# Moving the shift columns of the first gate product into its rows, spreading norm factors without diagonals, and a second spread for the final scaling

## The chip, the cores and the metric

One core of one Trainium2 chip runs the whole program; seven cores are idle. The metric is the device time of one execution in microseconds (us). The engines are named as in the profile: PE is TensorE (PEld its weight loads), DVE VectorE, ACT ScalarE, POOL GpSimd, SP SyncE, which here only issues DMAs.

## The reference

Two layers of a trunk run over 256 latent rows `h` and 256 context rows `hc` of width 2048. Layer 0 mixes by centred pooling, layer 1 by neighbourhood attention in which the latent queries also read the context. Every sub-layer begins with an RMS norm and a modulation, and each layer ends with a gated MLP of width 5504. After layer 1 only the latents go on.

```
def rms_norm(x, g):
    y = x * rsqrt(mean(x * x, axis=-1) + 1e-6)
    return y * g
def modulate(x, shift, scale):
    return x * (1 + scale) + shift
def conv_ffn(u, w_gate, w_up, conv_w, conv_b, w_down):
    gp = pad(u @ w_gate)
    gte = gp[:, :T] * conv_w[0] + gp[:, 1:T + 1] * conv_w[1] + gp[:, 2:] * conv_w[2] + conv_b
    return (silu(gte) * (u @ w_up)) @ w_down
...
h = h + ml[:, 2] * y_lat
h = h + ml[:, 5] * conv_ffn(modulate(rms_norm(h, norm2_g[i]), ml[:, 3], ml[:, 4]), ...)
...
return rms_norm(h, final_norm_g)
```

## The kernel before

**Layout.** The rows live in SBUF transposed: `hl` is [128, 16, 256], the 16 slices k being the 2048 features and the 256 columns the latent tokens (T = 256); `hc` is the same for the context. Every fp32 product is split: an operand x becomes hi = x rounded to FP32R and lo = x - hi, and a weight tile w is multiplied as w_hi by [x_hi | x_lo] (512 columns) and w_lo by x_hi (256 columns). Weights come in halves of 1024 columns. For each, SP issues a DMA into a staging tile, ACT casts the hi part (L150) and DVE, at times POOL, subtracts the lo part (L153). The hi and lo tiles of layer 1's MLP take turns in eight pairs of buffers, so a cast waits for the last product that read the same buffer eight halves earlier.

**Order.** The code is written as one stream. A scheduler that simulates the engines' times sets the order in which each engine's queue holds its instructions. `tc.high_priority()` and `tc.issue_after(x)` bend it, and the list `hold` puts weight casts behind named instructions. Each engine takes its queue in order.

**Norm factors.** The class `Norm` serves five norms: n1 and n2 in layer 0, n3 (latents and context, four chunks of 128 tokens) at the start of layer 1, n4 (latents) ahead of layer 1's MLP and n5 (latents) at the end. `add` squares a slice on ACT (L359) and sums up on DVE (L365). `totals` (L378) sums over partitions on PE with a column of ones, which gives one column per chunk with the token in the partition; DVE adds the partial sums (L382) and scales (L383); POOL raises to the power -1/2 (L387). `spread` then has to turn this column into a row that stands in all partitions: DVE multiplies the identity by the column, which makes a diagonal matrix `n4d` (L393), and PE multiplies it with a 128x128 matrix of ones (L395) into a PSUM bank `n4b`. `each` does the whole for n3, n4 and n5; `rstd` for n1 and n2.

**Layer 1's MLP, first block.** While the factor of n4 is being made, PE multiplies the first gate tile g_0 with raw rows, that is `hl` times (1 + scale) without the factor (`raw[k]`, made by L1015 on ACT and L1016 on DVE): 16 products of 512 columns (L1084) and 16 of 256 (L1088). The factor is applied to the result afterwards. The shift's share of g_0 is a column of its own. `shift_sums` multiplies the hi and lo weights with `sh` (the shift as hi and lo, two columns, made by L1021 and L1022) in 32 products of two columns (L1100), and DVE adds both columns into `gsh` (L1102). `norm_b` makes the normed rows `B[k]` (in the tiles `oA`) for all other products: DVE multiplies by the factor (`nrmB`, L1030); ACT casts hi (L1031); for even k DVE makes lo (L1037); for odd k ACT makes a copy `nrmBz` (L1034), and POOL makes lo from it (L1035). PE goes on with u_0, g_1 and u_1 over B[0], B[1] and so on.

**The attention's last stretch.** `x_tile` (L1424) makes the attention's output rows, `oA`, hi on ACT and lo on DVE. In the same stretch POOL copies bias rows (L1345) and multiplies for the rotary embedding (`rk`, `rq`, L1272).

**The end.** The last down product adds into `hl` (L1160, DVE). n5 squares each slice, and `final_gain` (L1132, ACT) multiplies it by the final gain, for the last four slices after n5's spread in the code. `rs` (L1193, ACT) is a copy of the factor for POOL, which scales slices 0 to 3 (L1197); DVE scales the other twelve out of PSUM (L1199), in four pieces; five DMAs write `out` (L1201).

Of the kernel before, what the change touches and what calls it, by code (L numbers as in the profile page):

```python
# [10 lines left out]
F32 = mybir.dt.float32  # L11
# [49 lines left out]
def kernel(ctx: ExitStack, tc: tile.TileContext, xT, cxT, wmod, wg, wu, wd, wp,  # L61
# [29 lines left out]
    ones = main.tile([P, P], F32, name="ones")  # L91
# [254 lines left out]
    class Norm:  # L346
# [24 lines left out]
        def totals(self):  # L371
            nj = self.n // P
            sqs = [self.acc] + self.last
            na = len(sqs)
            ps = bank("d", f"{self.name}s")
            for i, sq in enumerate(sqs):
                for j in range(nj):
                    ins = nc.tensor.matmul(ps[:, na * j + i : na * j + i + 1], sq[:, P * j : P * j + P], ones[:, 0:1],  # L378
                                           start=True, stop=True)
# [9 lines left out]
        def spread(self, v, js, pb):  # L389

            dg = self.pool.tile([P, 512], F32, tag="t2", name=f"{self.name}d{js[0]}")
            for i, j in enumerate(js):
                self.diag = nc.vector.tensor_scalar(dg[:, P * i : P * i + P], ident, v[:, j : j + 1], None, op0=ALU.mult).ins  # L393
            n = P * len(js)
            self.cast = nc.tensor.matmul(pb[:, :n], ones, dg[:, :n], start=True, stop=True).ins  # L395
# [603 lines left out]
    with ExitStack() as ph2:  # L999
# [12 lines left out]
        for k in range(KT):  # L1012
            a = raw[k] = rows[k][:, 1]
            with n4.urgent(k):
                nc.scalar.activation(a[:, 0], hl[:, k, :], AF.Copy, scale=M(1, 4, k, 0))  # L1015
                nc.vector.scalar_tensor_tensor(a[:, 1], hl[:, k, :], M(1, 4, k, 0), a[:, 0].bitcast(F32),  # L1016
                                               op0=ALU.mult, op1=ALU.subtract)
        sh = f1.tile([P, KT, 2], F32R, bufs=1, name="sh")
        for k in range(0, KT, 4):
            v = modT[1, 12 + k // 4][:, :, 0]  # L1020
            nc.scalar.copy(sh[:, k : k + 4, 0], v)  # L1021
            nc.vector.tensor_tensor(sh[:, k : k + 4, 1], v, sh[:, k : k + 4, 0].bitcast(F32), op=ALU.subtract)  # L1022
# [3 lines left out]
        def norm_b(ks):  # L1026
            for k in ks:
                a = rows[k][:, 0]
# [13 lines left out]
        def gu1(f):  # L1042
            res = []
            if f == 0:
# [14 lines left out]
                gu_b(ps, early[0, "g"], raw, (n4.last_sum, n4.cast))  # L1059
                shift_sums(early[0, "g"], n4.cast)  # L1060
# [32 lines left out]
        def shift_sums(parts, behind):  # L1093

            ps = bank("d", "gsh")
            with tc.issue_after(behind):
                for k in range(KT):
                    c = P * (k % 8)
                    for j, w in enumerate(parts[k // 8]):
                        nc.tensor.matmul(ps[:, 0:2], w[:, c : c + P], sh[:, k, :], start=(k == 0 and j == 0),  # L1100
                                         stop=(k == KT - 1 and j == 1))
            nc.vector.tensor_reduce(out=gsh, in_=ps[:, 0:2], axis=AX.X, op=ALU.add)  # L1102

        def gate1(f, banks):
            res = []
            for nm, ps in zip("gu", banks):
                e = f1.tile([P, 512], F32, tag="t2", name=f"e{nm}_{f}")[:, 0:T]
                with tc.high_priority() if f == 0 and nm == "g" else ExitStack():
                    nc.scalar.copy(e, ps[:, T:])
                    ins = nc.vector.tensor_tensor(e, e, ps[:, :T], op=ALU.add)  # L1110
                if f == 0 and nm == "g":
                    hold.append(ins.ins)
                    nc.vector.tensor_tensor(e, e, rstd[:, 0:T], op=ALU.mult)
                    nc.vector.tensor_scalar(e, e, gsh, None, op0=ALU.add)
# [21 lines left out]
        def down1(c, fs, acts, after=None):  # L1136
            n = len(fs)
            last = c == len(chunks) - 1
            for mg in range(4):
                parts = split(load(lambda a, b: wd[1, mg, :, fs[0] + a // 512 : fs[0] + b // 512, :], 512 * n, f"wd1_{c}_{mg}"),  # L1140
                              f"wd1_{c}_{mg}")
                for m in range(4):
# [15 lines left out]
                    if last:  # L1158
# [4 lines left out]
                        if k < KT - 4:  # L1163
# [29 lines left out]
        nc.scalar.copy(rs[:, 0], rstd[:, 0:T])  # L1193
        for j, (a, b) in enumerate(((0, 4), (4, 6), (6, 8), (8, 12), (12, 16))):
            v = hl[:, a:b, :]
            if j == 0:
                nc.gpsimd.tensor_tensor(v, v, rs[:, 0:1, :].broadcast_to([P, b - a, T]), op=ALU.mult)  # L1197
            else:
                nc.vector.tensor_tensor(v, v, rstd[:, 0:T].unsqueeze(1).broadcast_to([P, b - a, T]), op=ALU.mult)  # L1199
        for a, b in ((4, 6), (6, 8), (8, 12), (0, 4), (12, 16)):  # L1200
            nc.sync.dma_start(out[:, a:b, :], hl[:, a:b, :])  # L1201
# [27 lines left out]
def _attention(tc, ap0, bank, ld, A, M, hl, wq, wv, wo, rope, band, ident, v_first):  # L1229
# [9 lines left out]
    with ExitStack() as es:  # L1239
# [184 lines left out]
        def x_tile(k):  # L1424
            rows[k] = ap0.tile([P, 2, 2, T], F32R, tag=f"A{k}", name=f"oA{k}")
            a = rows[k][:, 0]
            nc.scalar.copy(a[:, 0], O[k])
            nc.vector.tensor_tensor(a[:, 1], O[k], a[:, 0].bitcast(F32), op=ALU.subtract)
# [152 lines left out]
```

## Time and profile before

| what | value |
|---|---|
| median of 3 runs | 3029.84 us (3027.93 to 3030.15) |
| profiled execution: its time, its span | 3030.79 us, 3029.0 us |
| PE busy | 2970.9 us (98% of the span), 14878 matmuls |
| DVE, ACT, POOL busy | 67%, 45%, 29% |
| mean granted clock of TensorE | 0.994 |
| bytes moved by DMA | 572.32 MB, mean 189 GB/s |

The span is the time from the first to the last instruction of the profiled execution; 1.8 us of the execution's time lie outside it. "Busy" counts an instruction from its start to its end; PE's instructions overlap in the pipeline, so the pace of a row of products is read from their starts. In the chain of waits, a piece is the time that an instruction adds to the path that ends last. The granted clock is the share of TensorE's full clock that its throttle let through.

### The profile page before, as it was taken

What the parts mean: (1) busy time and instruction counts of PE and PEld (TensorE: products, weight loads), DVE (VectorE), ACT (ScalarE), POOL (GpSimd) and SP (SyncE); (2) the same over time, 40 slices, a digit from 0 to 9 for tenths busy, and PEclk for the clock granted to TensorE, in tenths of its full rate; (3) what the DMA queues carried; (4) which work ended last, traced back from release to release, by engine and by line L of the source; (5) the groups of instructions that cost most, each with busy time, mean ns of one, the idle gap of its engine ahead of it and who ended that gap; (6) DMA issues with size and microseconds to landing.
All of it is one profiled execution on the core that took longest, in us unless ns stands there. A gap on an engine that the chain in (4) does not pass through costs nothing.

```text
span 3029.0 us, 40973 instructions
## 1 busy us (share of the span) xinstructions
PE 2970.9 (98%) x14878; PEld 2401.6 (79%) x14878; DVE 2036.5 (67%) x2921; ACT 1354.3 (45%) x2225; POOL 865.6 (29%) x864
## 2 busy tenths in 40 slices
PE   6999999999999999999999999999999999999998
PEld 2655678887888888888887888888888888888887
DVE  5455887566786867687776666474877666666666
ACT  3333573323333233333334444353556666566665
POOL 1011310312314030231412111010101565566665
PEclk9999999999999999999999999999999999999999
DMA  9988535555875867786782333333346565555553
GB/s 386 338 298 324 195 104 175 161 172 168 245 207 184 263 178 231 209 241 193 220 244 87 115 108 117 100 114 99 118 161 200 176 195 194 188 181 188 184 185 112
DMA packets 224779, 572.32 MB, mean 189 GB/s; under 512 B 55232, under 2 KB 68032, under 8 KB 224576
## 3 DMA queue, kind: packets, MB, share of 16 engines
q1 hardware_dynamic: 224576, 569.70, 58.3%
q8 instruction: 117, 1.92, 0.2%
q14 instruction: 86, 0.70, 0.1%
HBM read 563.32 MB, written 11.53 MB: 190 GB/s over the span
## 4 chain that ended last, share of the span: by engine, by line
PE 93%; DVE 3%; issue 1%; ACT 1%; DMA 1%; POOL 0%; DVEq 0%; ACTq 0%; POOLq 0%
PE u L1084 5%; PE g L1084 5%; PE d L931 5%; PE d L933 5%; PE d L932 5%; PE d L1152 5%; PE u L896 4%; PE u L894 4%; PE u L895 4%; PE g L896 4%; PE g L895 4%; PE g L894 4%; PE u L1088 3%; PE g L1088 3%; PE d L1156 3%; PE mod L195 2%
## 5 line engine op out<-in xcount | busy, mean ns | idle before, releaser
L952 POOL TENSOR_TENSOR hl<-hl,dy 128x256 f32<-128x256 f32 x144 | 141.3, 981 | 942.8 <-ACT dy L949 679.1
L1169 POOL TENSOR_TENSOR hl<-hl,dy 128x256 f32<-128x256 f32 x320 | 313.1, 1010 | 234.8 <-ACT dy L1167 231.8
L282 DVE SCALAR_TENSOR_TENSOR macc<-wm,sc,macc 128x512 f32<-128x512 f32 x360 | 262.6, 781 | 6.7 <-DMA wm<-wmod 6.3
L260 DVE SCALAR_TENSOR_TENSOR macc<-wm,sc,macc 128x1024 f32<-128x1024 f32 x120 | 162.5, 1354 | 89.4 <-DMA wm<-wmod 88.4
L949 ACT ACTIVATE dy<-d,modT 128x256 f32<-128x256 f32 x224 | 93.6, 471 | 141.1 <-PE d L933 134.9
L952 POOL TENSOR_TENSOR hc<-hc,dy 128x256 f32<-128x256 f32 x144 | 143.6, 997 | 0.0
L1167 ACT ACTIVATE dy<-d,modT 128x512 f32<-128x512 f32 x160 | 104.7, 685 | 57.5 <-PE d L1156 57.1
L1345 POOL COPY bias<-rows 128x160 f32<-128x160 f32 x64 | 35.9, 563 | 304.4 <-DVE nm L1354 151.3
L195 PE MATMUL mod<-wm,sc 128*32 128x512 f32 x640 | 96.1, 606 | 22.1 <-DMA wm<-wmod 22.1
L153 DVE TENSOR_TENSOR wd_3l<-wd,wd_3h 128x1024 fp32r<-128x1024 f32 (+1 forms) x44 | 55.6, 1267 | 80.2 <-ACT wd_3h L150 80.1
L501 ACT ACTIVATE sg<-g 128x512 f32<-128x512 f32 x43 | 27.3, 634 | 149.6 <-DVE g L498 149.2
L153 DVE TENSOR_TENSOR wd_2l<-wd,wd_2h 128x1024 fp32r<-128x1024 f32 (+1 forms) x44 | 58.8, 1347 | 47.8 <-ACT wd_2h L150 47.8
L588 POOL TENSOR_TENSOR pf<-ws,inv 128x256 f32<-128x256 f32 x32 | 28.5, 912 | 198.3 <-DVE ws L580 140.4
L153 DVE TENSOR_TENSOR wd_1l<-wd,wd_1h 128x1024 fp32r<-128x1024 f32 (+1 forms) x44 | 55.9, 1273 | 36.8 <-ACT wd_1h L150 36.8
L150 ACT CAST wd_0h<-wd 128x1024 fp32r<-128x1024 f32 (+1 forms) x44 | 45.2, 1030 | 61.7 <-PE g L895 48.9
L150 ACT CAST wd_1h<-wd 128x1024 fp32r<-128x1024 f32 (+1 forms) x44 | 45.0, 1026 | 56.1 <-PE u L1084 29.7
L195 PEld LDWEIGHTS mod<-wm,sc 128*32 128x32 f32 x640 | 18.0, 109 | 64.8 <-issue 35.6
L931 PE MATMUL d<-act,wd_0h 128*128 128x512 f32 x172 | 67.4, 396 | 1.0 <-ACT dy L949 1.0
L931 PE MATMUL d<-act,wd_3h 128*128 128x512 f32 x172 | 68.2, 396 | 0.0
L932 PE MATMUL d<-act,wd_2h 128*128 128x512 f32 x172 | 68.1, 396 | 0.0
L933 PE MATMUL d<-act,wd_0l 128*128 128x512 f32 x172 | 67.9, 395 | 0.0
L933 PE MATMUL d<-act,wd_2l 128*128 128x512 f32 x172 | 67.9, 395 | 0.0
(1711 smaller groups left out, 9374.1 us busy)
## 6 DMA issues: line engine op xcount, KB each, us to landing
wm<-wmod SPq DMA_DIRECT2D x384, 512.0 KB, 6.2
wd<-wd SPq DMA_DIRECT2D x168, 512.0 KB, 4.5
wg<-wg SPq DMA_DIRECT2D x156, 512.0 KB, 4.4
wu<-wu SPq DMA_DIRECT2D x156, 512.0 KB, 4.6
wv<-wv SPq DMA_DIRECT2D x32, 512.0 KB, 3.9
wk<-wq SPq DMA_DIRECT2D x32, 512.0 KB, 3.8
wq<-wq SPq DMA_DIRECT2D x32, 512.0 KB, 3.7
wo<-wo SPq DMA_DIRECT2D x32, 512.0 KB, 4.3
```

The source lines that it names most:

```text
L195: nc.tensor.matmul(ps[32 * j : 32 * j + 32, :], sc[:, at : at + 32], ts[j // 2][0][:, 512 * (j % 2) : 512 * (j % 2) + 512], start=(c == 0 ...
L282: nc.vector.scalar_tensor_tensor(acc[:, s], w, sc2[:, k, s : s + 1], acc[:, s], op0=ALU.mult, op1=ALU.add)
L894: nc.tensor.matmul(ps, hi[:, c : c + P], xh, start=(k == 0), stop=False)
L895: nc.tensor.matmul(ps, hi[:, c : c + P], xl, start=False, stop=False)
L896: nc.tensor.matmul(ps, lo[:, c : c + P], xh, start=False, stop=(k == KT - 1))
L931: nc.tensor.matmul(ps, hi[:, o : o + P], xh, start=(i == 0), stop=False)
L932: nc.tensor.matmul(ps, hi[:, o : o + P], xl, start=False, stop=False)
L933: nc.tensor.matmul(ps, lo[:, o : o + P], xh, start=False, stop=(i == n - 1))
L952: nc.gpsimd.tensor_tensor(h_of(s)[:, k, :], h_of(s)[:, k, :], y[:, s], op=ALU.add)
L1084: nc.tensor.matmul(ps, hi[:, c : c + P], flat(x[k]), start=(k == 0), stop=False)
L1088: nc.tensor.matmul(ps[:, T:], lo[:, c : c + P], x[k][:, 0], start=False, stop=(k == KT - 1))
L1169: nc.gpsimd.tensor_tensor(hl[:, k, :], hl[:, k, :], y[:, q], op=ALU.add)
```

## The change

1. `ones` is one column, [128, 1].
2. `spread` makes no diagonal. PE multiplies with the column v, repeated 128 times, as the stationary matrix and the identity as the moving one, 128 columns a chunk.
3. `each` sums, reduces and raises to the power pair by pair of chunks, each pair in a bank of its own.
4. `shift_sums` and the `sh` tile are gone. Row tiles `oA` are two columns longer. Behind the raw hi rows stand two columns, hi and lo of the shift, written by POOL in `x_tile` (32 instructions of one column). `g_raw` multiplies w_hi with [raw hi | 2 columns], w_hi with raw lo, and w_lo with [raw hi | 2 columns]: 258, 256 and 258 columns.
5. `gate1` for g_0 takes `gsh` from the two columns behind its result, has no two halves to add, and adds `gsh` on ACT.
6. At the end, the last six final gains stand in one block on ACT behind n5's last square. A second spread, `n5c`, goes to a bank of its own, from which ACT copies `rs`. POOL scales slices 12 to 15, DVE the others in five pieces of 1, 1, 2, 4 and 4 slices, each followed by its DMA; the DMA of slices 12 to 15 stands last in the code.

```diff
-    ones = main.tile([P, P], F32, name="ones")
+    ones = main.tile([P, 1], F32, name="ones")
...
         def spread(self, v, js, pb):
-            dg = self.pool.tile([P, 512], F32, tag="t2", name=f"{self.name}d{js[0]}")
             for i, j in enumerate(js):
-                self.diag = nc.vector.tensor_scalar(dg[:, P * i : P * i + P], ident, v[:, j : j + 1], None, op0=ALU.mult).ins
-            n = P * len(js)
-            self.cast = nc.tensor.matmul(pb[:, :n], ones, dg[:, :n], start=True, stop=True).ins
+                self.cast = nc.tensor.matmul(pb[:, P * i : P * i + P], v[:, j : j + 1].broadcast_to([P, P]), ident,
+                                             start=True, stop=True).ins
             return pb
...
         def each(self):
             with tc.high_priority():
-                v = self.totals()
-                for i in range(0, self.n // P, 2):
-                    self.power(v[:, i : i + 2])
-                return [self.spread(v, range(i, i + 2), bank("d", f"{self.name}b{i}")) for i in range(0, self.n // P, 2)]
+                pairs = range(0, self.n // P, 2)
+                sqs = [self.acc] + self.last
+                na = len(sqs)
+                ps = {i: bank("d", f"{self.name}s{i}") for i in pairs}
+                todo = [(a, i) for a in range(na) for i in pairs]
+                if len(pairs) == 2:
+                    todo[3:5] = todo[4:2:-1]
+                for a, i in todo:
+                    for j in range(2):
+                        ins = nc.tensor.matmul(ps[i][:, na * j + a : na * j + a + 1], sqs[a][:, P * (i + j) : P * (i + j) + P],
+                                               ones, start=True, stop=True)
+                self.last_sum = ins.ins
+                vs = self.v = {}
+                for i in pairs:
+                    v = vs[i] = main.tile([P, 2], F32, name=f"{self.name}v{i}")
+                    nc.vector.tensor_reduce(out=v, in_=ps[i][:, 0 : 2 * na].rearrange("p (j a) -> p j a", a=na), axis=AX.X,
+                                            op=ALU.add)
+                    self.diag = nc.vector.tensor_scalar(v, v, 1.0 / D, EPS, op0=ALU.mult, op1=ALU.add).ins
+                    self.power(v)
+                return [self.spread(vs[i], range(2), bank("d", f"{self.name}b{i}")) for i in pairs]
...
-                gu_b(ps, early[0, "g"], raw, (n4.last_sum, n4.cast))
-                shift_sums(early[0, "g"], n4.cast)
+                g_raw(ps, early[0, "g"])
...
-        def shift_sums(parts, behind):
-            ps = bank("d", "gsh")
-            with tc.issue_after(behind):
-                for k in range(KT):
-                    c = P * (k % 8)
-                    for j, w in enumerate(parts[k // 8]):
-                        nc.tensor.matmul(ps[:, 0:2], w[:, c : c + P], sh[:, k, :], start=(k == 0 and j == 0),
-                                         stop=(k == KT - 1 and j == 1))
-            nc.vector.tensor_reduce(out=gsh, in_=ps[:, 0:2], axis=AX.X, op=ALU.add)
+        def g_raw(ps, parts):
+            for j, behind in enumerate((n4.last_sum, n4.cast)):
+                ks = range(8 * j, 8 * j + 8)
+                for k in ks:
+                    w = parts[j][0][:, P * (k % 8) : P * (k % 8) + P]
+                    nc.tensor.matmul(ps[:, : T + 2], w, raw[k][:, : T + 2], start=(k == 0), stop=False)
+                    nc.tensor.matmul(ps[:, :T], w, raw[k][:, T + 2 :], start=False, stop=False)
+                with tc.issue_after(behind):
+                    for k in ks:
+                        nc.tensor.matmul(ps[:, : T + 2], parts[j][1][:, P * (k % 8) : P * (k % 8) + P], raw[k][:, : T + 2],
+                                         start=False, stop=(k == KT - 1))
...
-                        if k < KT - 4:
+                        if k < KT - 6:
                             final_gain(k)
...
+        with tc.issue_after(n5.done):
+            for k in range(KT - 6, KT):
+                final_gain(k)
         rstd = n5.each()[0]
-        for k in range(KT - 4, KT):
-            final_gain(k)
-        rs = f1.tile([P, 2, T], F32, tag="t2", name="rs5")
-        nc.scalar.copy(rs[:, 0], rstd[:, 0:T])
...
+        rs = f1.tile([P, 512], F32, tag="t2", name="rs5")[:, 0:T]
+        with tc.high_priority():
+            nc.scalar.copy(rs, n5.spread(n5.v[0], range(2), bank("gu", "n5c"))[:, 0:T])
+        g = hl[:, 12:16, :]
+        nc.gpsimd.tensor_tensor(g, g, rs.unsqueeze(1).broadcast_to([P, 4, T]), op=ALU.mult)
+        for a, b in ((0, 1), (1, 2), (2, 4), (4, 8), (8, 12)):
             v = hl[:, a:b, :]
...
+            nc.vector.tensor_tensor(v, v, rstd[:, 0:T].unsqueeze(1).broadcast_to([P, b - a, T]), op=ALU.mult)
+            nc.sync.dma_start(out[:, a:b, :], v)
+        nc.sync.dma_start(out[:, 12:16, :], g)
...
         def x_tile(k):
-            rows[k] = ap0.tile([P, 2, 2, T], F32R, tag=f"A{k}", name=f"oA{k}")
-            a = rows[k][:, 0]
+            row = ap0.tile([P, 4 * T + 2], F32R, tag=f"A{k}", name=f"oA{k}")
+            a = row[:, 0 : 2 * T].rearrange("p (s t) -> p s t", s=2)
+            rows[k] = a, row[:, 2 * T :]
             nc.scalar.copy(a[:, 0], O[k])
+            v, c = M(1, 3, k, 0), row[:, 3 * T : 3 * T + 2]
+            nc.gpsimd.tensor_copy(c[:, 0:1], v)
+            nc.gpsimd.tensor_tensor(c[:, 1:2], v, c[:, 0:1].bitcast(F32), op=ALU.subtract)
```

The engines' queues change in these places. A row names the line, the operation, what it writes and reads, and the shape; the line numbers of the changed kernel are 10 to 20 higher. First PE's queue of before, from the spread of n4 to the first product over a normed row (six of the eight L1088 rows and all but two of the 32 L1100 rows are left out):

```order
L395 MATMUL n4b_18739<-n4d_18740,ones 128x256
L1088 MATMUL g_0_18781<-oA_17710,wg_0l_18754 128x256
...
L1088 MATMUL g_0_18781<-oA_17950,wg_0l_18754 128x256
L1100 MATMUL gsh<-sh,wg_0h_18749 128x2
...
L1100 MATMUL gsh<-sh,wg_0l_18754 128x2
L1084 MATMUL u_0_18940<-oA_17686,wu_0h_18761 128x512
```

And PE's queue of the changed kernel at the same place:

```order
L1109 MATMUL g_0_18798<-oA_17976,wg_0h_18770 128x256
L392 MATMUL n4b_18758<-ident,n4v_18754 128x128 x2
L1112 MATMUL g_0_18798<-oA_17722,wg_0l_18771 128x258
...
L1112 MATMUL g_0_18798<-oA_17976,wg_0l_18771 128x258
L1093 MATMUL u_0_18939<-oA_17682,wu_0h_18778 128x512
```

Nothing stands between the last raw product and the first normed one any more. Next ACT's queue of before from the last casts of tile 1's weights on (`wg_2h` are the two halves of the next gate tile):

```order
L150 CAST wu_1_1h_18936<-wu_1_1024_18930 128x1024
L1031 ACTIVATE oA_17686<-nrmB_18848,modT_86 128x256
L1031 ACTIVATE oA_17689<-nrmB_18852,modT_86 128x256
L1034 ACTIVATE nrmBz_18855<-nrmB_18852,modT_86 128x256
L1031 ACTIVATE oA_17692<-nrmB_18858,modT_86 128x256
L1031 ACTIVATE oA_17695<-nrmB_18862,modT_86 128x256
L1034 ACTIVATE nrmBz_18865<-nrmB_18862,modT_86 128x256
L150 CAST wg_2h_19077<-wg_2_0_19073 128x1024
```

And the same of the changed kernel:

```order
L150 CAST wu_1_1h_18935<-wu_1_1024_18929 128x1024
L150 CAST wg_2h_19076<-wg_2_0_19072 128x1024
L150 CAST wg_2h_19080<-wg_2_1024_19074 128x1024
L1041 ACTIVATE oA_17682<-nrmB_18847,modT_86 128x256
L1041 ACTIVATE oA_17687<-nrmB_18851,modT_86 128x256
```

Both casts of wg_2 have moved ahead of the first cast of a normed row. Last POOL's queue of the changed kernel in the attention's last stretch; of before there stand only the `bias`, `rk` and `rq` rows, in the same order:

```order
L1361 COPY bias_13467<-rows_0_17667 128x4x40
L1446 CAST oA_17682<-modT_86 128x1
...
L1288 TENSOR_TENSOR rk_17564<-rk_17564,rp 128x256
L1447 TENSOR_TENSOR oA_17692<-modT_86,oA_17692 128x1
...
L1447 TENSOR_TENSOR oA_17976<-modT_86,oA_17976 128x1
L1361 COPY bias_13469<-rows_1_17779 128x4x40
L1361 COPY bias_13467<-rows_0_17845 128x4x40
L1288 TENSOR_TENSOR rq_17625<-rq_17625,rp 128x256
```

Six of the 32 instructions of one column stand ahead of that `rk`, and 26 between it and the next `bias`. Elsewhere, at the end, PE has the two products of `n5c` ahead of those of `n5b`, and SP's queue has the DMA of slices 12 to 15 fourth of six, ahead of those of slices 4 to 7 and 8 to 11. At n3 the sums of the latent pair stand at places one, three and five of six.

More of the change, by code (lines that the diff above doesn't have):

```diff
@@ L1012 @@
         for k in range(KT):
-            a = raw[k] = rows[k][:, 1]
+            a = raw[k] = rows[k][1]
+            hi, lo = a[:, 0:T], a[:, T + 2 :]
             with n4.urgent(k):
-                nc.scalar.activation(a[:, 0], hl[:, k, :], AF.Copy, scale=M(1, 4, k, 0))
-                nc.vector.scalar_tensor_tensor(a[:, 1], hl[:, k, :], M(1, 4, k, 0), a[:, 0].bitcast(F32),
+                nc.scalar.activation(hi, hl[:, k, :], AF.Copy, scale=M(1, 4, k, 0))
+                nc.vector.scalar_tensor_tensor(lo, hl[:, k, :], M(1, 4, k, 0), hi.bitcast(F32),
                                                op0=ALU.mult, op1=ALU.subtract)
[L1018 to L1022, printed above, removed]
         rstd = n4.each()[0]
@@ L1107, in gate1 @@
                 e = f1.tile([P, 512], F32, tag="t2", name=f"e{nm}_{f}")[:, 0:T]
-                with tc.high_priority() if f == 0 and nm == "g" else ExitStack():
-                    nc.scalar.copy(e, ps[:, T:])
[L1110 to L1114, printed above, removed]
+                if f == 0 and nm == "g":
+                    with tc.high_priority():
+                        nc.scalar.copy(e, ps[:, :T])
+                        nc.vector.tensor_reduce(out=gsh, in_=ps[:, T : T + 2], axis=AX.X, op=ALU.add)
+                        ins = nc.vector.tensor_tensor(e, e, rstd[:, 0:T], op=ALU.mult)
+                    hold.append(ins.ins)
+                    nc.scalar.activation(e, e, AF.Identity, bias=gsh)
+                else:
+                    nc.scalar.copy(e, ps[:, T:])
+                    nc.vector.tensor_tensor(e, e, ps[:, :T], op=ALU.add)
                 res.append(e)
```

12 lines of the change are left out of this document (3 added, 9 removed).

## The prediction

> **What bounds the kernel now.** I read the page first, then the chain of waits, then the timeline of each engine and the windows around the places that the change touches. The page:
>
> ```profile
> PE 2970.9 (98%) x14878; PEld 2401.6 (79%) x14878; DVE 2036.5 (67%) x2921; ACT 1354.3 (45%) x2225; POOL 865.6 (29%) x864
> ```
>
> PE bounds the kernel. The change takes no large product away, so what it is worth is read where PE works badly or stands still. The first such place is n4, in the chain of waits (start, us, piece):
>
> ```profile
> 2289.37 0.43 PE n4b L395 x2
> 2289.80 0.94 PE g L1088 x8
> 2290.75 4.68 PE gsh L1100 x32
> 2295.43 0.64 PE u L1084
> 2296.06 0.43 PE g L1084
> ...
> 2299.82 0.23 PE g L1084
> ```
>
> The 32 products of two columns stand on the path with 4.68 us, 0.146 us each, while a product of 256 columns beside them takes 0.94/8 = 0.118 us. Behind them a product of 512 columns takes 0.43 us, and from 2299.82 on 0.23. Why, the windows show (busy us of each engine, then PEclk, the granted clock):
>
> ```profile
> 2291.00:2293.00 2.00, 2.00 (x19) 2.00 (x18) 2.00 (x7) 2.00 (x6) 0.81 (x2) 0.94 0.63 223
> 2293.00:2295.40 2.40, 2.40 (x13) 2.40 (x12) 0.85 (x3) 2.40 (x6) 0.98 (x2) 0.50 0.04 7
> 2297.00:2299.00 2.00, 2.00 (x6) 1.52 (x6) 2.00 (x3) 1.35 (x4) 1.78 (x2) 0.50 0.07 8
> ```
>
> The clock falls to 0.50 in the midst of `gsh`, though PE counts as busy, and stays there for some four us of dense products.
>
> **First gate product (n4).** Two terms. First, the start of u_0, now at 2295.43. In the changed kernel `g_raw` ends where L1088 ends, 2289.80 + 0.94 = 2290.74, plus about 0.1 (32 products of 256 or 258 columns at 0.118 in place of 16 of 512 at 0.23): 2290.85. The 64 extra columns in all cost under 0.05 by the same pace; the longer row may cost more if odd widths are slower, which no row shows. Then u_0 needs the normed row 0:
>
> ```profile
> 2289.84 1.65 DVE L1030 SCALAR_TENSOR_TENSOR nrmB<-hl,modT,n4b 128x256 f32<-128x256 f32 x4 [0.42 <-PE n4b L395]
> 2291.41 0.48 DVE L1037 SCALAR_TENSOR_TENSOR oA<-nrmB,modT,oA 128x256 fp32r<-128x256 f32 x1
> ...
> 2295.46 0.16 DVE L1102 TENSOR_REDUCE gsh<-gsh 128x1 f32<-128x2 f32 x1 [1.61 <-PE gsh L1100]
> ...
> 2296.72 1.22 DVE L153 TENSOR_TENSOR wu_0l<-wu,wu_0h 128x1024 fp32r<-128x1024 f32 x1
> ```
>
> ```profile
> 2287.04 1.04 ACT L150 CAST wu_0h<-wu 128x1024 fp32r<-128x1024 f32 x1
> 2287.99 1.05 ACT L150 CAST wu_1h<-wu 128x1024 fp32r<-128x1024 f32 x1
> 2290.35 0.91 ACT L1031 ACTIVATE oA<-nrmB,modT 128x256 fp32r<-128x256 f32 x2 [1.32 <-DVE nrmB L1030]
> ...
> 2292.76 1.03 ACT L150 CAST wg_2h<-wg 128x1024 fp32r<-128x1024 f32 x1
> ```
>
> n4b's time is set by PE's own queue, so the missing diagonals gain nothing here: DVE starts `nrmB` at about 2289.85 as before. ACT used to wait 1.32 us for it; now the two casts of wg_2 fill that gap. They overwrite the buffers of wg_0's halves, whose hi parts are read for the last time at 2289.37. So ACT runs 2289.04 + 2 x 0.95 (the two rows above start 0.95 apart) = 2290.95, then row 0's hi until 2291.4, DVE's L1037 until 2291.9, which is where row 0 was ready before too (2291.41 + 0.48). u_0 starts at 2292.0, after 1.15 us of idle PE: **3.4 us** earlier. Second, the clock: from 2295.43 to 2299.82 there stand ten products, 4.39 us; at 0.23 each they take 2.3, so **2.1 us** go if the clock holds. Against that, later rows. POOL makes row 1:
>
> ```profile
> 2291.74 0.74 POOL L1035 TENSOR_TENSOR oA<-nrmBz,oA 128x256 fp32r<-128x256 f32 x1 [3.97 <-ACT nrmBz L1034]
> ```
>
> With ACT 0.55 late (2290.9 for 2290.35) it is ready at 2293.0, while PE has three products of row 0, 0.7 us, until 2292.7: 0.3 of waiting. Row 6 stands behind a weight split of 1.22 us in DVE's queue: after row 0 come six `nrmB` (0.41 each), the lo parts of rows 2, 4 and 6 (0.4 each, paced) and the split, 4.9 us, until 2296.8. PE wants it after six rows, 18 x 0.23 + 0.3 later than 2292.0, at 2296.4: another 0.4. After that the lo products give cover of several us. Net 3.4 + 2.1 - 0.7 = **4.8 us**; between 2.7 (clock falls anyway) and 5.5 (no new wait). DVE's wait of 1.61 us for `gsh` goes with it, which is part of why rows 4 to 6 come in time.
>
> Does 1.15 us of idle PE keep the clock? Two places in the trace stand on either side:
>
> ```profile
> 2206.00:2208.00 2.00, 0.64 (x8) 0.35 (x4) 0.51 (x4) 1.16 (x6) 0.00 (x0) 1.00 0.00 0
> 2208.00:2210.00 2.00, 2.00 (x14) 1.86 (x15) 1.58 (x7) 1.49 (x2) 0.00 (x0) 1.00 0.00 0
> ```
>
> ```profile
> 396.00:398.00 2.00, 0.56 (x2) 0.48 (x3) 2.00 (x5) 1.89 (x5) 0.00 (x0) 1.00 0.00 0
> 398.00:400.00 2.00, 2.00 (x7) 1.57 (x6) 2.00 (x3) 1.52 (x4) 1.99 (x2) 0.59 0.04 8
> ```
>
> 1.36 us without a matmul (2.00 - 0.64) left 1.00; 1.44 us of them, in another place, was followed by 0.59. Ours is shorter than both, so I take the clock as kept. The Trainium skill's page "TensorE: Matmul & The Clock Gate" (HAM oscillation) warns only of gaps over some 3.4 us; by it our gap would be free, but so would `gsh`, which was no gap at all, and there the trace disagrees with 0.50.
>
> **Spread and pairs (n3).** The chain:
>
> ```profile
> 1651.10 2.64 PE n3s L378 x24
> 1654.22 0.72 POOL n3v L387
> 1654.96 0.49 DVE n3d L393 x2
> 1655.59 1.21 PE n3b L395 x2
> ```
>
> The diagonal and its hand-over lie between 1654.94 and 1655.59: 0.6 saved. The latents' sums end two of twelve products earlier, 2 x 0.22 = 0.44, since their pair has places one, three and five. n3b as two products of 128 columns moves as many columns; starting earlier, it meets a higher clock: 0 to 0.6, I take 0.25. Together **1.3 us**, between 0.5 (the repeated stationary eats half) and 1.7. The context's pair follows on PE before the first v product needs it.
>
> **n1 and n2.** From the waits of PE, and beside it the longest wait of the attention:
>
> ```profile
> PE o L1380 <- DVE pt L1367: 1.8, 1, 1.8
> ...
> PE n2b L395 <- DVE n2d L393: 1.3, 1, 1.3
> ```
>
> n2: 0 (DVE sets the pace behind it) to 1.3; I take **0.7**, as DVE also loses the diagonal's work. n1, from the chain:
>
> ```profile
> 25.01 1.04 POOL n1v L387
> ...
> 28.16 10.16 DMA wm<-wmod
> ```
>
> Ten us of weight transfer follow n1b, which hide most of the diagonal: **0.2**, up to 0.9 if the transfers are asked for earlier. The scheduler also reorders scores and transposes in the attention, with the same work; I cost that at 0, between +1.8 and -1.8, the one wait of that size there.
>
> **The end (n5).** The chain, then the timeline and a window:
>
> ```profile
> 3018.60 0.49 DVE n5d L393 x2
> 3019.14 0.71 PE n5b L395 x2
> 3019.87 0.38 ACT rs L1193
> ```
>
> ```profile
> 3020.28 3.55 DVE L1199 TENSOR_TENSOR hl<-hl,n5b 128x512 f32<-128x512 f32 x4 [1.20 <-ACT rs L1193]
> 3020.32 2.35 POOL L1197 TENSOR_TENSOR hl<-hl,rs 128x1024 f32<-128x1024 f32 x1 [1.76 <-ACT rs L1193]
> ```
>
> ```profile
> 3024.00:3026.00 2.00, 0.00 (x0) 0.00 (x0) 0.00 (x0) 0.00 (x0) 0.00 (x0) 0.50 1.03 408
> ```
>
> Without diagonals the spread starts at 3018.6. Both spreads, n5c first, take about 0.7 as n5b did, so DVE starts at 3019.4, 0.9 earlier, with a bank of its own. ACT's block of six gains (about 0.4 each) runs until 3019.2, `rs` until 3019.6, POOL until 3022.0. But SP's queue has POOL's DMA fourth, so three pieces of 0.5 MB leave only after 3022; at 408 GB/s they take 3.9 us. The last bytes then come about 0.6 earlier than before: **0.6 us**, between 0 and 1.4.
>
> **Sum.** 4.8 + 1.3 + 0.7 + 0.2 + 0.6 = 7.6. Against the profiled execution, 3030.79 (span 3029.0 and 1.8 around it), that is 3023.2; it lay 0.95 above the median of the runs, so I forecast 3022.2. 0.2%, about what a measurement of this kernel can tell from no change, is 6.06 us, down to 3023.8.
>
> **Rivals.**
> (a) The clock falls at n4 although the gap is short: 2.1 us lost, 3024.3. For it speaks the row at 396 to 400, against it 2206 to 2210. The same skill page (Part 1, What's actually happening) has a free-running window, by which a gap's place and not its length alone would decide. Chance 0.20.
> (b) The casts of wg_2 on ACT hold row 0 back. If the second waits until the lo products end (2290.85), u_0 starts 1.5 us later, PE idles 2.7 us, and the clock falls: 3.6 lost, 3025.8. The buffer's last reader speaks against it. Chance 0.10.
> (c) The change doesn't do what it says: a repeated column as stationary costs PE what the diagonal cost DVE. Then 0.6 at n3, n2's 0.7, n1's 0.2 and the end's 0.6 go: 3024.3. Chance 0.08.
> (d) Slower: POOL's instructions of one column. Their price is not in the trace.
>
> ```profile
> 2171.26 0.98 POOL L1272 TENSOR_TENSOR rk<-rk,rp 128x256 f32<-128x256 f32 x1 [2.87 <-DVE rk L1271]
> 2178.11 1.07 POOL L1345 COPY bias<-rows 128x160 f32<-128x160 f32 x2 [5.87 <-issue]
> 2184.99 0.77 POOL L1272 TENSOR_TENSOR rq<-rq,rp 128x256 f32<-128x256 f32 x1 [5.81 <-DVE rq L1271]
> ```
>
> 26 of them stand between that rk (until 2172.24) and the two bias copies, and rq must start at 2184.99. They have 2184.99 - 2172.24 - 1.07 = 11.7 us, 0.45 each: from there on they hold up q's rotation, and so PE. At 1.04, the power of 128x4 above, they take 27 us: 15.3 late, so 3037.5. At 0.3 to 0.4, which I estimate from the bias copies (0.54 for 160 columns), they are covered. Chance 0.05.
>
> The forecast keeps 0.57. Faster by over 0.2% holds in most of it (0.53) and at the near edge of (a) and (c) (0.10): 0.63. Slower is (d) alone, less its near part: 0.04. Within 0.2%: 0.33. The range goes from 3018.0 (n4 5.5, n3 1.7, n2 1.3, the end 1.4 and a share of the rest) to 3027.5 (beyond (b), with the attention 1.8 worse); it leaves out (d) and the tails.
>
> **What would show it.** Right: no L1100 group; u_0 at about 1.2 us after the last L1112, granted clock 1.00 there; at n3 no DVE instruction between the power and n3b, and the latents' power before the last sum's end plus 0.5; DVE's last pieces starting 0.9 us earlier after the last square. Wrong: 0.50 after 2291 (a); ACT idle before the second wg_2h (b); an n3b over 1.2 us (c); POOL's `rq` late and PE waiting for scores (d).

## The result and the profile after

The changed kernel takes 3052.01 us (median of 6 runs, 3047.34 to 3052.98); the kernel before took 3031.35 beside it (6 runs, 3027.93 to 3035.41). The ratio is 1.0065, 95% interval 1.0054 to 1.0076: slower by 0.65%, about 20 us, where the forecast was 7.6 us faster and its range ended at 3027.5. The profiled execution of the changed kernel took 3052.75 us, span 3050.9.

PE's row of the page has eight matmuls more than before and 22 us more of busy time, so the time did not go into waiting:

```profile
PE 2993.0 (98%) x14886; PEld 2397.7 (79%) x14886; DVE 2030.1 (67%) x2902; ACT 1354.6 (44%) x2222; POOL 875.2 (29%) x896
```

The place that the forecast was about looks as it said. PE's timeline around n4 (start, us, instruction; in brackets the idle time before and who ended it), then ACT's, then the windows (busy us by engine, then the granted clock):

```profile
2315.01 0.61 PE L392 MATMUL n4b<-ident,n4v 128*128 128x128 f32 x4
2315.38 1.20 PE L1112 MATMUL g<-oA,wg_0l 128*128 128x258 f32 x8
2317.86 0.47 PE L1093 MATMUL u<-oA,wu_0h 128*128 128x512 f32 x1 [1.28 <-DVE oA L1047]
```

```profile
2314.68 2.00 ACT L150 CAST wg_2h<-wg 128x1024 fp32r<-128x1024 f32 x2
2316.58 0.90 ACT L1041 ACTIVATE oA<-nrmB,modT 128x256 fp32r<-128x256 f32 x2
```

```profile
2316.60:2318.00 1.40, 0.14 (x1) 0.17 (x2) 1.40 (x4) 1.40 (x5) 0.05 (x1) 1.00 0.30 120
2318.00:2320.00 2.00, 2.00 (x8) 1.36 (x9) 2.00 (x6) 2.00 (x6) 1.44 (x2) 1.00 0.05 8
```

No `gsh` products are left, the two casts of wg_2 stand ahead of row 0, u_0 starts 2.85 us after n4b (before: 2295.29 - 2289.21 = 6.08), PE idled 1.28 us, and the clock stayed at 1.00. All that arrives 25.8 us late. Where the delay came in is read from the starts of the same instructions in both traces:

```
place (start of)                     before    after   difference
first cg product                       72.7     77.9    +5.3
n2b                                   348.1    353.9    +5.7
first product with wg_8               397.4    403.2    +5.8
last down product of layer 0         1650.7   1670.7   +20.0
first v product                      1658.1   1677.1   +19.0
first op product                     2177.6   2204.0   +26.5
n4b                                  2289.2   2315.0   +25.8
first down product of layer 1        2381.4   2403.1   +21.7
last product of n5s                  3017.1   3039.6   +22.4
end of the span                      3029.0   3050.9   +21.9
```

Three stretches lose: the first 78 us (5.3), layer 0's MLP (14.2) and the attention's projections (7.5 from v to op). The change adds no columns to any of them (n1's spread is four products of 128 columns where it was one of 512). In the MLP PE is busy all the time in both kernels, and does less. One window of 50 us before:

```profile
600.00:650.00 50.00, 50.00 (x220) 41.17 (x220) 47.58 (x67) 13.79 (x16) 0.00 (x0) 1.00 0.66 213
```

and after:

```profile
600.00:650.00 50.00, 50.00 (x216) 40.32 (x216) 47.13 (x66) 13.70 (x16) 0.00 (x0) 1.00 0.65 205
```

216 products where there were 220, at the same clock. One line's gate products of one weight tile, before (duration min/median/max in ns, first and last start):

```profile
L894 PE MATMUL g<-A,wg_10h x16: 389/389/389, 488.6 to 498.8; 128*128 128x512 f32 x16
```

and after:

```profile
L908 PE MATMUL g<-A,wg_10h x16: 391/396/398, 495.0 to 505.5; 128*128 128x512 f32 x16
```

The 45 products between the first and the last start took 10.2 us and take 10.5. Mean distance from one start to the next, over whole lines and without the distances over 400 ns, in ns:

```
products                                 before            after
layer 0 gate and up, L894 to L896        228.9 228.4 229.1 234.1 231.8 233.0   (3360 products)
v, L1224 to L1226                        228.1 227.8 226.9 233.6 232.5 232.4   (768 products)
layer 0 down, L931 to L933               231 to 233        231 to 233
```

4.2 ns more on 3360 products are 14 us of the 14.2. What slowed are the products that read row tiles (`A`); the down products read other buffers and kept their pace. The one thing that the change did to `A` is its size: all row tiles of slice k share one buffer, `x_tile` now asks for 4104 bytes of it and not 4096, and the buffers stand 4128 bytes apart.

### The profile page after: what moved, and what is told of

It reads as the page before. It is cut to its first block, busy times and chain, and to the rows that moved or that the text cites. A ratio compares the mean times of both kernels' runs of the same rounds, so it can differ in the third digit from the quotient of the medians.

```text
span 3050.9 us, 41025 instructions
## 1 busy us (share of the span) xinstructions
PE 2993.0 (98%) x14886; PEld 2397.7 (79%) x14886; DVE 2030.1 (67%) x2902; ACT 1354.6 (44%) x2222; POOL 875.2 (29%) x896
## 4 chain that ended last, share of the span: by engine, by line
PE 91%; issue 4%; DVE 3%; ACT 1%; POOL 0%; DMA 0%; SPq 0%; DVEq 0%; POOLq 0%; ACTq 0%
PE u L1093 5%; PE d L945 5%; PE d L947 5%; PE d L946 5%; PE g L1093 5%; PE d L1166 5%; PE u L910 4%; PE u L908 4%; PE u L909 4%; PE g L910 4%; PE g L908 4%; PE g L909 4%; PE u L1097 3%; PE g L1097 3%; PE d L1170 2%
## 5 line engine op out<-in xcount | busy, mean ns | idle before, releaser
L966 POOL TENSOR_TENSOR hc<-hc,dy 128x256 f32<-128x256 f32 x144 | 136.9, 951 | 0.0
L945 PE MATMUL d<-act,wd_1h 128*128 128x512 f32 x172 | 67.9, 395 | 0.0
```

The source lines that it names most:

```text
L945: nc.tensor.matmul(ps, hi[:, o : o + P], xh, start=(i == 0), stop=False)
L966: nc.gpsimd.tensor_tensor(h_of(s)[:, k, :], h_of(s)[:, k, :], y[:, s], op=ALU.add)
```

## The experiments

In the expectations, theory A is this size and place of the row tiles; B is the shrunken `ones`, behind which the row and weight buffers move by 448 bytes (`ident` and `hl` by 480); C is the new order of the instructions. A1 and A2 are two forms of A: the distance of the row's start from the start of the weights modulo 512 bytes, and starts at odd multiples of 32 bytes.

**e1_rows_4096.** The kernel before with the change's `Norm` class, its `ones` of one column and its end; the rows and the 32 shift products are those of before.

> The kernel before with the one-column ones, the spread without diagonals, the sums by pairs and the new end, but with rows of 4096 bytes, the sh tile and the 32 products of two columns. Theory A (the longer rows move all 16 row tiles against the weight buffers, and products that read them run at 233 ns instead of 227): about 3 us under before (n2 1.2, n3 1.3, the end 0.5), L894 back at 227 to 229 ns. Theory B (the slower pace comes from the shorter ones tile, which moves ident, hl and all that follows by 480 bytes): about 17 us over before, L894 at 233. Theory C (the new order of the engines' queues): somewhere between, with L894 slow as in after.

3035.36 us (3029.48 to 3038.17), ratio to before 1.0009, interval 0.9999 to 1.0019. The layers run at the pace of before (221 products from 600 to 650 us). B and C fall as causes of the 14 us. The 3 us under before that were forecast did not come: the median lies 5.2 us above, with six of the ten runs over 3035, and in the profiled execution, one of these, 4.6 us are lost ahead of the first cg product (77.3, before 72.7).

**e2_rows_4104.** e1 with two columns in each row tile that nothing uses:

```diff
-rows[k] = ap0.tile([P, 2, 2, T], F32R, tag=f"A{k}", name=f"oA{k}")
+row = ap0.tile([P, 4 * T + 2], F32R, tag=f"A{k}", name=f"oA{k}")
+rows[k] = row[:, 0 : 4 * T].rearrange("p (a s t) -> p a s t", a=2, s=2)
```

> As e1_rows_4096, with two unused columns at the end of every row tile (slots 4128 bytes apart instead of 4096). Theory A: 17 to 20 us slower than e1, 12 of them in layer 0's MLP, L894 at 232 to 234 ns. Theories B and C: as e1 within 2 us.

3057.61 us (3055.63 to 3059.07), ratio 1.009 (1.0075 to 1.0105), 22.3 us over e1. No instruction is added to e1 or taken from it. A holds: eight unused bytes a row are the whole loss in the layers. In the window:

```profile
600.00:650.00 50.00, 50.00 (x216) 40.32 (x215) 46.98 (x67) 13.70 (x16) 0.00 (x0) 1.00 0.62 205
```

**e3_gap_128.** e1 with 128 unused bytes ahead of the rows:

```diff
+gapp = ctx.enter_context(tc.tile_pool(name="gapp", bufs=1))
+gapp.tile([P, 32], F32, name="gap")
 ap0 = ctx.enter_context(tc.tile_pool(name="ap0", bufs=1))
```

> As e1_rows_4096, with 128 unused bytes ahead of the row tiles: slots stay 4096 apart and at multiples of 64, but every row stands 384 of 512 bytes off the three weight buffers that stood in phase with it, and the others stay 128 off. If what counts is the distance of row and weight addresses modulo 512 (A1): 15 to 20 us slower than e1, L894 at 232 to 234. If it is rows at odd multiples of 32 bytes (A2): as e1 within 2 us.

3045.45 us (3038.81 to 3051.6), ratio 1.005 (1.0033 to 1.0068), 10 over e1. A2 falls, since 128 is no odd multiple of 32 and yet slow. The direction is A1's, the size is less than it asked for. Two things in its trace work against the loss. The gap also moves the act buffers, to 256 bytes from the first weight buffers modulo 512 (128 in e1), and the down products of layer 0 become faster, 226.8 to 227.0 ns from start to start (231 to 233 in e1), while the gate and up products take 233.2 to 233.4 (228.4 to 228.8). One group of the down products in e1:

```profile
L945 PE MATMUL d<-act,wd_3h 128*128 128x512 f32 x172 | 68.2, 396 | 0.0
```

and in e3:

```profile
L947 PE MATMUL d<-act,wd_3h 128*128 128x512 f32 x172 | 67.2, 391 | 0.0
```

And the clock stays at 1.00 behind the 32 products of two columns, where before, e1, e2 and e4 fall to 0.50; from n4b to the first down product of layer 1 there are 90.0 us and not 93.2 (e1):

```profile
2312.00:2314.00 2.00, 2.00 (x15) 1.82 (x15) 1.59 (x6) 2.00 (x5) 0.58 (x2) 1.00 0.00 0
```

**e4_aligned.** e1 with 384 unused bytes behind the rows. That leaves rows and the first three weight buffers where they are and moves all later buffers, so that every weight, row and act buffer starts at the same address modulo 512 (192).

> As e1_rows_4096, with 384 unused bytes behind the row tiles, which brings the five further weight buffers and the activation tiles of both layers to the same place modulo 512 as rows and first weight buffers. A1: 12 to 22 us faster than e1, L931 (down products of layer 0) at 227 to 229 ns instead of 232, L1084 the same. A2, B and C: as e1 within 2 us.

3015.27 us (3013.44 to 3017.3), ratio 0.9951 (0.9936 to 0.9966): 20 us under e1 and 15 under before. A1 holds also in the direction that no kernel had tried; from 600 to 650 us there are now

```profile
600.00:650.00 50.00, 50.00 (x222) 41.40 (x222) 47.57 (x67) 13.85 (x16) 0.00 (x0) 1.00 0.64 212
```

222 products, two more than before. The gate and up products go 226.7 to 226.8 ns apart (228.4 to 228.8 in e1, where one of layer 0's four pairs of weight buffers stood 128 bytes off). The down products gain too (389 to 391 ns each in the groups, 392 to 396 before). No row has moved against e1, so it is not the row's address by itself that counts.

**e8_gap_256.** As e3, with 256 bytes.

> e1_rows_4096 with 256 unused bytes ahead of the rows: the distance of rows to the three first weight buffers modulo 512 becomes 256 in place of 0 (it was 128 in e3_gap_128), all other distances modulo 512 (128 and 0) stay as in e1 and e3. If the pace goes by the distance modulo 512 and any distance but 0 is slow: as e3, 3045. If it goes by the distance modulo 256: as e1, 3035.

3031.23 us (3029.03 to 3036.95), ratio 1.0005 (0.9996 to 1.0014), and 221 products from 600 to 650 us. 256 bytes are as good as 0, so A1 is mended: what counts is the distance modulo 256.

**e9_pace.** The pace by itself.

```
for r in range(n):
    a, b = step(r)
    nc.tensor.matmul(ps[:, :cols], w[:, a : a + P], mv[:, b : b + cols], start=(r == 0), stop=(r == n - 1))
```

> The disputed cost by itself; the kernel computes nothing of the backbone, it only runs chains of 160 fp32r products of 128x128 weights with 512 columns (three chains: 256), one after another, weights and rows in two buffers at one address modulo 512; its time is no comparison. In chains by_a to by_p the rows start 0, 32, 64 ... 480 bytes further than the weights modulo 512; zero repeats by_a; four and sixteen are 4 and 16 bytes off; half_a, half_c, half_e have 256 columns at 0, 64 and 128 bytes. Theory (pace goes by the distance modulo 256): by_a, by_i (256 bytes) and zero at 227 ns a product, by_e and by_m (128, 384) at about 232.5, those between at 232 to 234; 160 products 36.3 against 37.2 us. Rival 1: only 128 and 384 are slow and other multiples of 32 or 64 are not. Rival 2: the pace has nothing to do with these addresses and comes from the other engines' traffic: all chains at 227. Which weight counts: in own, each product's rows lie at the distance 0 to its own weights and 128 to the weights loaded next; in next, the other way about. If rows being read disturb the load of the next weights, own is slow and next is fast; if a product's own weights count, the reverse.

Groups of instructions (busy us of 160 products, mean ns of one):

```profile
L78 PE MATMUL four<-mv,w 128*128 128x512 f32 x160 | 38.0, 399 | 0.0
L78 PE MATMUL by_f<-mv,w 128*128 128x512 f32 x160 | 37.6, 396 | 0.0
...
L78 PE MATMUL by_e<-mv,w 128*128 128x512 f32 x160 | 37.5, 395 | 0.0
...
L78 PE MATMUL next<-mv,w 128*128 128x512 f32 x160 | 37.0, 392 | 0.0
L78 PE MATMUL by_c<-mv,w 128*128 128x512 f32 x160 | 36.8, 391 | 0.0
L78 PE MATMUL by_k<-mv,w 128*128 128x512 f32 x160 | 36.8, 391 | 0.0
L78 PE MATMUL own<-mv,w 128*128 128x512 f32 x160 | 36.7, 390 | 0.0
L78 PE MATMUL by_i<-mv,w 128*128 128x512 f32 x160 | 36.5, 389 | 0.0
L78 PE MATMUL zero<-mv,w 128*128 128x512 f32 x160 | 36.5, 389 | 0.0
L78 PE MATMUL by_a<-mv,w 128*128 128x512 f32 x160 | 36.4, 389 | 0.0
```

By the starts a product takes 226.7 to 226.8 ns at a distance of 0 or 256 (by_a, by_i, zero), 229.0 at 64 and 320 (by_c, by_k), 234.3 at 160 and 416, 233.3 to 233.4 at all other multiples of 32, 231.7 at 16 and 236.6 at 4 bytes. The two halves of 0 to 512 repeat each other, and no other engine works: rivals 1 and 2 fall. The three chains of 256 columns take 117.8 to 120.0 ns with no such order. Which product's weights count stays open: own (228.4) and next (230.1) both lie between fast and slow.

**e6_after_aligned.** The changed kernel with rows of 4096 bytes, the gap of e4 and a pad in the place of the `sh` tile.

```diff
-row = ap0.tile([P, 4 * T + 2], F32R, tag=f"A{k}", name=f"oA{k}")
+row = ap0.tile([P, 4 * T], F32R, tag=f"A{k}", name=f"oA{k}")
...
-hi, lo = a[:, 0:T], a[:, T + 2 :]
+if k % 2 == 0:
+    los = f1.tile([P, 2, T], F32R, tag="act", bufs=8, name=f"lo_{k}")
+hi, lo = a[:, 0:T], los[:, k % 2]
```

> The changed kernel with rows of 4096 bytes: the two shift columns take the place of the first two columns of the raw lo part, the lo parts of two rows go into one of the act buffers that are still unused then, and 384 bytes lie empty behind the rows, so that every weight, row and act buffer starts at one address modulo 512. All other edits of the change stand. Theory A1 (distance of the two operands modulo 512): all that the changed kernel lost after 80 us comes back, and the first gate product brings its 4 us over e4_aligned (3015.3): 3009.5 to 3012.5. Rival (the shift columns cost what they bring, by the 258 columns or by one-column instructions on GpSimd): 3015 to 3017. If something else of the change costs time beside the addresses: above 3020.

3007.51 us (3005.81 to 3013.24), ratio to before 0.992 (0.9907 to 0.9934): the change with its rows in place is 22.6 us faster than before, some 43 faster than as it was written (each against the runs of before beside it), and 7.8 faster than e4. From n4b to the first down product of layer 1 it needs 87.6 us (e4: 93.0), 5.4 less. The profiled executions differ by another 5.3 us at the start (first cg product at 72.2, in e4 at 77.5), which varies from run to run, so the 7.8 is no clean figure for the change. Nothing else in the change costs time that shows.

**The start.** The first cg product came 4.5 to 5.3 us late in the changed kernel and e1 to e4. PE's timeline of the changed kernel:

```profile
22.06 3.58 PE L378 MATMUL n1s<-ones,n1q 128*128 128x1 f32 x16
25.56 3.63 PE L195 MATMUL mod<-wm,sc 128*32 128x512 f32 x12
29.12 2.08 PE L392 MATMUL n1b<-ident,n1v 128*128 128x128 f32 x8
...
47.15 2.08 PE L618 MATMUL pm<-ph,wp0h 128*128 128x512 f32 x4 [3.21 <-ACT ph L609]
```

and of before:

```profile
22.30 2.22 PE L378 MATMUL n1s<-ones,n1q 128*128 128x1 f32 x16
24.45 2.16 PE L195 MATMUL mod<-wm,sc 128*32 128x512 f32 x16
27.00 1.13 PE L395 MATMUL n1b<-n1d,ones 128*128 128x512 f32 x2 [0.40 <-DVE n1d L393]
```

The same 16 sums take 3.58 us or 2.22: TensorE works at half its pace until about 31 us in one (the one-column sums start 0.213 us apart there, n1b's products as far) and until 22.9 in the other (0.111 apart from then on), although the windows show a granted clock of 1.00 in both. n1b comes two us later, and the first pooling product three, behind an idle time of 3.21 us.

**e5_n1_spread.** Before, with the new spread for n1 alone.

```diff
+if self.name == "n1":
+    for i, j in enumerate(js):
+        self.cast = nc.tensor.matmul(pb[:, P * i : P * i + P], v[:, j : j + 1].broadcast_to([P, P]), ident, ...)
+    return pb
```

> Question: the changed kernel and all four runs so far reach the first cg product about 5 us later than the one profile of before (72.7 us), because n1b comes at 29 us and not at 27 and the matmuls between 23 and 30 us run at the slow pace. This kernel is before with one edit: n1's spread reads a repeated column and writes no diagonal; nothing else, and no address, moves. Theory S1 (the new spread of n1, with the order on TensorE that it brings, makes the start slow): n1b at 29 us, first cg at 77 to 78, median 4 to 5 us above before. Rival S2 (when TensorE becomes fast in the first 30 us varies from run to run, and is the same lottery for every kernel; before's profile had luck): n1b at 27 or 29 by chance, median within 2 us of before, and both spread over the same 8 us.

3034.91 us (3028.42 to 3035.77), ratio 1.0007 (0.9999 to 1.0016). The profiled execution, 3030.34, has n1b at 26.30 and the first cg product at 72.6, as before. So this edit does not make every start late. But the times fall into two heaps, 3027 to 3030.5 and 3033 to 3036; 10 of 12 runs lie in the upper, of before 10 of 23, and the median lies 4.8 us above before, where S1 had put it and S2 had not. S2 holds in that both kernels have both heaps; whether the new order makes the late start more frequent stays open.

**e7_after_aligned_n1d.** e6 with n1's diagonal back.

> e6 with the diagonal back in n1's spread alone (the matrix of ones in a scratch buffer of the first stage). S1: the start is as in before, n1b at 27 us, first cg at 73, and the time 4 to 5 us under e6: about 3006. S2: the same as e6 within 2 us.

3007.87 us (3005.84 to 3013.41), ratio 0.9921 (0.9907 to 0.9935): the same as e6, with one run over 3013 of four in each. S1, by which it would be 4 to 5 us under e6, is not borne out; four runs each cannot tell whether late starts become rarer.

**e10_warm.** e6 with unused products ahead of the first mod product.

```diff
 n1.add(h_of, k)
+if k < 15:
+    nc.tensor.matmul(warm, ident, hl[:, k : k + 2, :].rearrange("p a b -> p (a b)"), start=True, stop=True)
```

> e6_after_aligned with 15 products that nothing uses, of the identity with the latents as they arrive, ahead of the first mod product: TensorE works from 8 to about 17 us and not only from 18.7. Theory S2 (what differs between runs is when TensorE's fast pace begins, 23 or 30 us, and a late begin costs 5 us): no late begin is left, n1s takes 2.2 us or less in the profile, n1b stands at 26 us or before, all runs lie between 3005 and 3009, none at 3013. Rival (the late begin comes from something else, such as when the first weights arrive): one to two of the runs stay at 3012 to 3014. If the products delay the first mod product, all runs are 1 to 2 us later.

3008.51 us (3007.79 to 3012.2), ratio 0.9924 (0.991 to 0.9937). The unused products took too long, 0.86 us each where I had reckoned with half:

```profile
8.34 14.76 PE L546 MATMUL warm<-hl,ident 128*128 128x512 f32 x30 [8.34 <-DMA hl<-xT]
23.03 1.07 PE L197 MATMUL mod<-wm,sc 128*32 128x512 f32 x8
24.03 1.95 PE L380 MATMUL n1s<-ones,n1q 128*128 128x1 f32 x16
```

The first mod product came 4.3 us later than in e6, and n1b came at 28.60, where 26 or earlier was expected. n1s was fast, as expected, and yet one of the five runs, 3012.2, lies where the rival had put one or two and S2 none; with the delay in it, the run decides nothing about S2. It shows one thing: TensorE was slow from 8.34 on (starts 0.85 us apart) and fast from 11.78 on (0.43). The Trainium skill's page "TensorE: Matmul & The Clock Gate" (Part 1) gives about 3.4 us of work until the clock rises, in windows that run freely; the 3.44 us here agree, the 12 us (19.0 to 31) in the changed kernel do not.

**e11_warm_10.** Ten of them.

> e10_warm with 10 of the unused products in place of 15. In e10 they took the slow pace for 3.4 us (until 11.8) and then 0.86 each; 15 ended at 23.0, four us behind the time at which the first mod product is ready. 10 should end at 18.7 and delay nothing. Theory S2: n1s in 2.0 us, n1b at 25 to 26, first cg at 71 to 73, all runs between 3004.5 and 3007.5, 5 us and more between these and the late runs of e6 (3013.2). Rival (late runs come from something else): one run or more at 3012 to 3014.

3005.23 us (3003.6 to 3006.01), ratio to before 0.9911 (0.989 to 0.9932), the lowest median of the study; its interval overlaps that of e6. n1s took 1.95 us, n1b came at 25.28, and no run of the four is late; e6 and e7 together had two of eight, so this agrees with S2 and does not prove it. The first cg product stood at 73.5, later than forecast. The fast pace did not last either: n1b's products start 0.213 us apart again (0.112 in e6), and here the window shows it:

```profile
26.00:28.00 2.00, 2.00 (x11) 1.26 (x13) 0.00 (x0) 0.59 (x1) 0.00 (x0) 0.50 1.02 408
```

## Why the prediction was wrong

The step that failed is the sentence "The 64 extra columns in all cost under 0.05 by the same pace; the longer row may cost more if odd widths are slower, which no row shows." It priced the two columns only where they are multiplied, at `g_raw`, and in rival (d) where POOL writes them. At `g_raw` it was right: 32 products of 256 or 258 columns go 0.12 us apart (2313.08, 2313.20, 2313.32 ...). But a longer tile also moves every buffer behind it, and the same buffers hold the normed rows of layer 0 and of the attention. Before, they stood at the same address modulo 256 as the first three weight buffers (128 and 128 modulo 512); 4128 bytes apart, only every eighth does. That cost 22 us (e2 against e1), three times the gain that was forecast, in stretches for which I had written no term at all. None of the rivals held it; the slower one, POOL's small instructions, was not the cause (e2 has none of them and loses as much).

The terms themselves, in the changed kernel (and in e6, where the layers run undisturbed):

- **First gate product**, forecast 4.8 us: from n4b to the first down product of layer 1 there were 92.2 us and are 88.1, a gain of 4.1 (e6: 4.6). u_0 is 3.2 of it, forecast 3.4. The clock held, so rival (a) fell: the ten products from u_0 on take 2.6 us, before 4.4, which is 1.7 where 2.1 was forecast. Later waits and the slower pace took some 0.8 back, forecast 0.7. The second cast of wg_2 did not wait, so (b) fell.
- **n3**, 1.3: last down product to first v product 7.4 us before, 6.4 after, 1.0 gained (e6: 1.4).
- **n2**, 0.7: the 1.27 us that PE waited ahead of n2b are gone in both; about 1.2 gained, near the upper bound.
- **n1**, 0.2: within the noise of the start, which also decides between 5 us more or less.
- **The end**, 0.6: from the last n5s product 11.9 us before, 11.4 after. In e6 nothing is gained (12.0): the granted clock is 0.58 there (2995 to 2998) and the two spreads take 1.12 and 1.06 us in place of 0.71 and 0.69.
- **Rival (c)**, a spread as dear as the diagonal: n3 and n2 speak against it (n3b takes 2.07 us for both pairs, 2.04 before).
- **Rival (d)**, POOL's one-column instructions: they take 0.18 us alone, and 26 of them about 8 us:

```profile
2203.17 1.67 POOL L1446 CAST oA<-modT 128x1 fp32r<-128x1 f32 x5
2204.79 0.41 POOL L1447 TENSOR_TENSOR oA<-modT,oA 128x1 fp32r<-128x1 f32 x1
2205.15 0.18 POOL L1446 CAST oA<-modT 128x1 fp32r<-128x1 f32 x1
```

Five in 1.67 us are 0.33 each, under the 0.45 at which they would have held up q.

These gains add to 6.8 us (4.1 + 1.0 + 1.2 + 0.5), where 7.6 was forecast. The balance of the changed kernel's span: 5.3 at the start, 1.7 in the pooling, 14.2 in the MLP, 7.5 in the projections, 0.7 in layer 1's MLP, less 0.7 between op and n4b and less 6.8, which is the 21.9 us. Of the 20.7 us between the medians some 3 belong to the start, which differs from run to run: the changed kernel's one early run, 3047.34, lies 18 above the early runs of before (3028 to 3030).

What is shown: the loss in the layers follows the distance of rows and weights alone (e2, e3, e4, e8, e9), and the change brings its gain when that distance is kept (e6). What is argued: that the 5 us at the start are chance (e7 and the two heaps speak for it, e5's ten late runs of twelve and the late run of e10 do not). What is open: why TensorE's fast pace begins at 23 us in some runs and at 30 or 31 in others, and which product's weights make the conflict.

## What to carry to other kernels

Before a tile is made longer, look at what else lives in its buffer and at the addresses of everything allocated behind it: the price of two columns was not in the products that use them. For fp32r products of 512 columns on this chip keep row and weight buffers at one address modulo 256 bytes, by padding tiles or leaving a gap; 384 unused bytes brought 20 us here (e4 against e1). When a kernel loses time with no new waits and the same clock, count its products in a window of equal length, and compare paces from start to start before looking for a stall.

## What the hardware showed that was not expected

- An fp32r product of 128x128 with 512 columns takes 226.7 to 226.8 ns when its row starts at the weights' address modulo 256, 229.0 at 64 bytes from it, about 233 at other multiples of 32 and 236.6 at 4 bytes. With 256 columns (117.8 to 120.0 ns) it does not matter.
- 258 columns cost no more than 256 that shows: 0.12 us from start to start for both.
- TensorE can run at half its pace for 12 us of dense work at the start while the granted clock is listed as 1.00 (the changed kernel, 19.0 to 31); the pace of known products shows it, the column does not always (e11 lists 0.50 from 26 to 28).
- 32 products of two columns lost the clock in six of seven profiled executions (0.50 in before, e1, e2, e4, e5 and e8) and kept it in e3 (1.00). 1.28 us without any product kept it at n4 (1.00 in the changed kernel and e6), while at the end of e6 1.25 us without any were followed by 0.58. So neither the products nor the length of a gap decides by itself; what does is not shown.
